# Memory attention: the sample's pair scores in the other PSUM pool, the prompt's last turn ahead of the value products, the convolution's small loads behind the output projection's weights

## The chip, the cores and the metric

The kernel runs on one core of a Trainium2 chip. The metric is the device time of one execution in microseconds (us); of several runs the median is taken. Engines are named as the profile names them: PE (TensorE matmul), PEld (its weight loads), DVE (VectorE), ACT (ScalarE), POOL (GpSimd) and SP (SyncE, which here issues nearly all DMAs).

## What is computed

One layer of a hybrid decoder, for a prompt group (512 rows) and a sample group (8 sequences of 4 rows) with the same weights: a mixer (mLSTM and differential attention), cross-attention into 256 memory tokens, and a convolutional FFN. The change lies in the cross-attention and at its seam to the FFN. Cut to what matters there:

```
def mem_attend(h, mk, mv, w_mq, w_mo):            # 4 heads x 256
    q = (h @ w_mq).reshape(B, T, MEM_HEADS, MEM_HEAD_DIM)
    s = jnp.einsum('bqhd,bkhd->bhqk', q, mk) * (MEM_HEAD_DIM ** -0.5)
    p = jax.nn.softmax(s, axis=-1)
    o = jnp.einsum('bhqk,bkhd->bqhd', p, mv).reshape(B, T, D_MODEL)
    return o @ w_mo

def conv_ffn(h, conv_buf, w_up, w_dw, b_dw, w_down):
    u = h @ w_up
    ext = jnp.concatenate([conv_buf, u], axis=1)
    c = b_dw
    for j in range(CONV_W):                       # 3 taps
        c = c + ext[:, j:j + T] * w_dw[j]
    a, g = c[..., :D_FF], c[..., D_FF:]
    return (jax.nn.silu(g) * a) @ w_down
```

The prompt's keys and values are computed from its memory; the sample's eight sequences each read their own keys and values (`cache_mem_k`, `cache_mem_v`, 1 MB each per sequence).

## The kernel before, in words

All products are float32: each weight tile of 512 KB is loaded into a staging tile (`wst`), ACT casts its high part (L146) and DVE subtracts to get the low part (L147); the pair is a `wslot`, of which there are four. A prompt product is three matmuls: high by high (L411), high by low (L412), low by high (L413).

PSUM has eight banks in two pools: `psm`, five banks, for tiles made by `mmp()`, and `psa`, three banks, for tiles made by `at()`. A tile takes a bank when one is free, and its first writer waits for the last reader of the tile that had the bank.

The memory attention has two strands that are woven together on PE:

- The prompt, one generator `prompt` with steps over eight items (4 heads x 2 row halves). Step t runs `ch_out(t-3)` (the product with the values, tile `cpo`, then the split into the projection's operand `oT`, for every second item 12 matmuls), `ch_turn(t-2)` (four transposes, tile `cpt`, then the splits `pT`), and `ch_soft(t)` (scores, tile `sca`, then DVE's maximum `cnm`, ACT's exponential `cp`, DVE's scaling of `cp`).
- The sample: `mk_scores` for pairs of sequences (tile `ssc`, one per sequence, L1527, copied by ACT to `sc`, L1530), `mk_sum` and `mem_softmax` (tiles `pS`, `spc`, `spt`; the weights end in `caz`), and `mv_out`, the products with the sample's values (tile `pso`, L1593) in the order `VORD`: sequences 2, 1, 0, then 7, 6, 5, 4, 3. The values of sequences 0 to 2 lie in the six staging tiles that weights use, those of 3 to 6 in the four buffers that `wslot` uses, those of 7 elsewhere.

After that come the first half of the projection by `w_mo` (tile `mm`), the transposes `ost` of the sample's result, and the transposes `cvp` (L1688, L1692) of the convolution's taps and states, which 24 small DMAs (L1674 to L1676) have brought into the tile `cr`. `xb` are five loads of the residual rows (L1144).

The order on each engine is set when the program is built: a scheduler takes the instructions by priority (mostly the order in which the code issues them), with two overrides, `tc.high_priority()` and `tc.issue_after(ins)`, which puts a block's instructions behind `ins` on its engine. Each engine, and the DMA queue of SP, then runs its list in that order. SP's DMAs use eight semaphores in turn, so that each waits for the landing of the one eight before it. `W` plans the weight slots; `W.pump()` issues what the slots allow, here four tiles of `w_mo`.

Of the kernel before, what the change touches and what calls it, by code (L numbers as in the profile page):

```python
# [15 lines left out]
P = 128  # L16
# [61 lines left out]
def kernel(ctx: ExitStack, tc: tile.TileContext, I, O):  # L78
# [9 lines left out]
    KSTEPS, VLOADS, NMID, VSTEPS = (3, 7, 11, 15), (13, 15), 3, (0, 1, 3, 5, 6, 7)  # L88
# [25 lines left out]
    def at(name="at"):  # L114
        return psa.tile([P, 512], F32, name=name, tag="at")

    def mmp(name="mm"):
        return psm.tile([P, 512], F32, name=name, tag="mm")
# [8 lines left out]
    def v2(t, b):  # L127
        return t.rearrange("p (a b) -> p a b", b=b)
# [10 lines left out]
    dma = nc.sync.dma_start  # L139
# [4 lines left out]
    def split(hi, lo, src, eng=None):  # L144

        nc.scalar.copy(out=hi, in_=src)  # L146
        (eng or nc.vector).tensor_tensor(out=lo, in0=src, in1=f32(hi), op=SUB)  # L147

    def rows(b):
        return (b * P, P) if b < 4 else (SEQ, NS)  # L150
# [56 lines left out]
    W = Weights(NSLOT)  # L207

    def stage():
        return stg.tile([P, 1024], F32, name="wst", tag="st")  # L210

    def slot_tile():
        return wp.tile([P, 2, 1024], F32R, name="wslot", tag="W")
# [11 lines left out]
    def slotA(w, k0, n0, nrow=256, share=False):  # L225
        def emit():
            st, s = v2(stage(), 512), slot_tile()
            sv = s.rearrange("p l (k n) -> p l k n", k=2)
            r0 = k0 * P
            if nrow == 256:  # L230
                dma(out=st, in_=w[r0:r0 + 256, n0:n0 + 512].rearrange("(k p) n -> p k n", p=P))
                split_w(sv, st, share)
            else:
                dma(out=st[:, 0, :], in_=w[r0:r0 + P, n0:n0 + 512])
                for p0 in (0, 64):
                    dma(out=st[p0:p0 + 64, 1, :], in_=w[r0 + P:r0 + P + 64, n0:n0 + 512])
                split(sv[:, 0], sv[:, 1], st)
            return sv, st
        W.add(emit)
# [113 lines left out]
    class Fill:  # L353
# [8 lines left out]
        def run(self, amount=1e9):  # L362
            while amount > 0 and self.q:
                try:
                    amount -= next(self.q[0])
                except StopIteration:
                    self.q.pop(0)
# [303 lines left out]
    for c0, c1 in HALF:  # L671
        n = c1 - c0
        ps = mmp()
# [51 lines left out]
    ps = at("gtp")  # L725
# [3 lines left out]
    ps = at("gtp")  # L729
# [193 lines left out]
    ps = at("npt")  # L923
# [37 lines left out]
    ps = at("nT0")  # L961
# [34 lines left out]
    ps = at("nTt")  # L996
# [122 lines left out]
    def proj_add(xt, gname, src, gname2, dst, order=None, scale=None):  # L1119

        g = gbc(gname)
        y0, s0, xb, pend, ready, target, late = {}, {}, {}, [], [], [], []

        def ssq(b, y, nm):
            n = rows(b)[1]
            ss = sm.tile([P, 1], F32, name=nm, tag=nm, bufs=6)
            j = Z("sqj")
            ACT(out=j[:n], in_=y, func=AF.Square, scale=DM ** -0.5, accum_out=ss[:n])
            return ss[:n]

        def ev0(b, ps):
            n = rows(b)[1]
            z = y0[b] = T2([P, 512], "y0")[:n]
            if b == 4:
                sample_sum(ps, z)
                ps = z
            s0[b] = ssq(b, ps, "ssy0")
            VTT(out=z, in0=ps, in1=g[:n, :512], op=MUL)

        def before(b):  # L1140
            for c in [4, 0, 1, 2, 3] if scale else [b]:
                if c not in xb:
                    xb[c] = N("xb")[:rows(c)[1]]
                    dma(out=xb[c], in_=src(c))  # L1144

        def ev1(b, ps):
            c0, n = rows(b)
            z = T2([P, 512], "y1")[:n]
            if b == 4:
                sample_sum(ps, z)  # L1150
                ps = z
            ss = ssq(b, ps, "ssy1")
            VTT(out=z, in0=ps, in1=g[:n, 512:], op=MUL)
            STT(out=ss, in0=s0[b], scalar=EPS, in1=ss, op0=ADD, op1=ADD)
            rs = rstd(ss, n, 1, None)
            late.append((b, z, rs))
            if not scale:
                add(*late.pop(0))

        def add(b, z, rs):  # L1160
            c0, n = rows(b)
            x = xb[b]
            for i, z in enumerate((y0[b], z)):
                c = slice(512 * i, 512 * i + 512)
                STT(out=x[:, c], in0=z, scalar=rs, in1=x[:, c], op0=MUL, op1=ADD)  # L1165
            dma(out=dst[c0:c0 + n, :], in_=x)
            ready.append((x, n, c0))
            while len(ready) > LR:
                rows_of(*ready.pop(0))

        def rows_of(x, n, c0):
            if scale is None:
                pend.append((norm_rows(x, n, ACTROWS), n, gname2, target[0], c0, POOLQ))
                return
            pend.append((x, n, gname2, target[0], c0, POOLQ))
            rs = sm.tile([P, 1], F32, name="rsd", tag="rsd", bufs=5)
            VCP(out=rs[:n], in_=rstd(sumsq(x, n, Z("sqx").bitcast(BF16)[:n]), n, 1, DM))
            scale[1].append((rs[:n], c0, n))

        def mid():  # L1180
            if len(pend) > (0 if scale else LP):
                norm_turn(*pend.pop(0))
            if late:

                with tc.issue_after(scaled[0].ins) if late[0][0] == 2 else nullcontext():
                    add(*late.pop(0))

        def second(xt2):
            target.append(xt2)
            run(gemmA(xt, 8, [4, 0, 1, 2, 3], ev1, block_major=True, before=before, mid=mid, midk=1 if scale else MIDK))  # L1190
            while late:
                add(*late.pop(0))
            while ready:
                rows_of(*ready.pop(0))
            while len(pend) > 2:
                norm_turn(*pend.pop(0))
            return pend
        return gemmA(xt, 8, order or allb, ev0, block_major=order is not None, halves=True), second
# [10 lines left out]
    for b in range(4):  # L1209
        c = slice(b * P, b * P + P)  # L1210
# [86 lines left out]
    prompt = pipe(4 * H, da_soft, lambda i: None, da_turn, da_av, da_end)  # L1297
# [59 lines left out]
    ps = at("dat")  # L1357
# [32 lines left out]
    for q in range(2):  # L1390
        st = v2(stage(), 256)
        dma(out=st, in_=mk_d[:, 4 * q:4 * q + 4])
        split(mkT[0][:, 4 * q:4 * q + 4], mkT[1][:, 4 * q:4 * q + 4], st)
    for c in range(2):
        st = stage()
# [113 lines left out]
    def mk_scores(bs):  # L1509

        t = None
        ps = {b: mmp("ssc")[:, :256] for b in bs}
        for e in range(2):
            if e and bs[0] == 0:
                next(prompt)
                t = scored[0].ins
            for b in bs:
                o = ps[b][:, e * P:e * P + P].rearrange("p (h c t) -> p h c t", h=2, c=2)
                for c in range(2) if b < 3 else (None,):
                    for j in range(8):  # L1520
                        g = NS * (j % 4)
                        if c is None:
                            w, k = o[g:g + NS], view(kst[b][0], 512 * e + NS * j, [(256, 2), (DM, 2), (1, NS)])
                        else:
                            w, k = o[g:g + NS, :, c], view(kst[b][c], 512 * e + NS * j, [(256, 2), (1, NS)])
                        with burst(t):
                            t = mm(w, lhsT=qx[e][j // 4][:, j % 4, b].rearrange("p e g t -> p (e g t)"), rhs=k,  # L1527
                                   start=(j < 4), stop=(j >= 4)).ins
        for b in bs:
            nc.scalar.copy(out=sc[:, b], in_=ps[b])  # L1530
        return t
# [80 lines left out]
    prompt = steps()  # L1612
# [30 lines left out]
    mk_sum(t)  # L1643
    with tc.high_priority():
        mem_softmax()
    for _ in range(NMID):
        next(prompt, None)
    pso = mmp("pso")[:, :256]
    for n0 in (0, 512):
# [1 line left out]
    W.nslots = NSLOT  # L1651
    mv_out(VORD[:6])
    W.pump()
    next(prompt, None)
    next(prompt, None)
    mv_out(VORD[6:])
    run(prompt)
    oS = Z("oS")[:, :256]
    nc.scalar.copy(out=oS, in_=pso)
    ps = at("ost")  # L1660
    for e in range(2):
        tr(ps[:, e * P:(e + 1) * P], oS[:, e * P:(e + 1) * P], ident)
    ps = ps[:, :256].rearrange("p (e h n) -> p h e n", e=2, n=NS)
# [8 lines left out]
    def conv_in(t, p0, o, c0, n):  # L1672

        dma(out=t[p0:p0 + 16, o:o + n], in_=conv0[:, c0:c0 + n])  # L1674
        dma(out=t[p0 + 16:p0 + 19, o:o + n], in_=I["w_dw"][0][:, c0:c0 + n])
        dma(out=t[p0 + 19:p0 + 20, o:o + n], in_=I["b_dw"][:, c0:c0 + n])  # L1676


    cr = N("cr")
    for g in range(6):  # L1680
        conv_in(cr, 20 * g, 0, 896 * g + (64 if g > 2 else 0), 896)
    conv_in(cr, 0, 896, 2688, 64)
    conv_in(cr, 0, 960, 5440, 64)
    for t0 in (0, 4):
        ps = at("cvp")
        nt = min(4, 7 - t0)
# [4 lines left out]
    ps = at("cvp")  # L1691
# [33 lines left out]
    def spread(i):  # L1725
# [9 lines left out]
        if i == 0:  # L1735
# [3 lines left out]
                            scale=(rsb, rss))  # L1739
# [109 lines left out]
    for gi, js in enumerate(groups):  # L1849
# [49 lines left out]
        if not last:  # L1899
            behind = []  # L1900
            for n0 in (0, 512):
# [3 lines left out]
                ps = [mmp() for _ in range(4)]  # L1905
# [11 lines left out]
            ps = {n0: at("sdn") for n0 in (0, 512)}  # L1917
# [141 lines left out]
```

## Time and profile before

| what | value |
|---|---|
| median of 3 runs | 939.27 us (938.86 to 941.57) |
| the profiled execution | 938.97 us |
| its span, first to last instruction | 937.2 us |
| PE busy | 914.7 us (98% of the span) |
| mean granted TensorE clock | 0.994 |
| HBM traffic | 138 GB/s over the span |

A profile is one execution. A row of the timeline gives the start, the busy time, the engine, the line and the operands; in brackets stands the idle time of the engine before it and what ended that. `x12` means twelve instructions merged into one row; a float32 matmul that isn't split by the kernel has two records. On SP a row is the time of issuing, not of the transfer. In a table of stretches the columns are the stretch, its length, the busy time with the number of instructions, the granted clock, the share of busy DMA engines and GB/s.

### The profile page before, as it was taken

The page shows a single profiled execution, that of the slowest core. Times are in us where ns is not written, and L with a number is a line of the kernel's source. Part 1 is how long each engine was busy: PE and PEld are TensorE (multiplying, and loading weights), DVE is VectorE, ACT ScalarE, POOL GpSimd, SP SyncE. Part 2 cuts the span into 40 slices and gives each one's busy share as a digit, 9 for nine tenths or more (in the row PEclk, how much of TensorE's full clock was granted, in tenths as well). Part 3 has the DMA queues.
Part 4 walks back from the last instruction along what each step waited for, and adds up shares of the span by engine and source line. Part 5 has one row for each costly group of instructions (what it writes and reads, how often), then busy time and mean ns, then how long its engine had stood idle before and what let it go on. Part 6 is the DMA issues. An engine that isn't in the chain of part 4 may idle for free. (4 is left out here: it accounts for less than half of the span.)

```text
span 937.2 us, 17472 instructions
## 1 busy us (share of the span) xinstructions
PE 914.7 (98%) x6780; PEld 798.0 (85%) x6780; DVE 607.5 (65%) x1128; ACT 377.7 (40%) x728; POOL 223.4 (24%) x475
## 2 busy tenths in 40 slices
PE   8999999999999999999999999999999999999995
PEld 5899787879866778998767899889988998999974
DVE  5845144565887438687545778637747785776767
ACT  5745233344586447724434533332212222222232
POOL 6611000024442116581000553001100110110114
PEclk9999999999999999999999999999999999999998
DMA  8950023335780439956766632062054304412023
GB/s 282 320 182 5 1 90 138 91 105 159 246 294 7 137 117 299 321 189 232 283 231 166 202 116 69 26 180 69 22 140 133 89 10 116 133 49 90 24 94 118
DMA packets 120834, 130.59 MB, mean 139 GB/s; under 512 B 8599, under 2 KB 86264, under 8 KB 120752
## 3 DMA queue, kind: packets, MB, share of 16 engines
q1 hardware_dynamic: 114568, 125.96, 42.5%
q10 hardware_dynamic: 6184, 3.53, 1.2%
q8 instruction: 53, 0.87, 0.4%
q14 instruction: 29, 0.24, 0.1%
HBM read 112.54 MB, written 16.93 MB: 138 GB/s over the span
## 5 line engine op out<-in xcount | busy, mean ns | idle before, releaser
L146 ACT CAST wslot<-wst 128x1024 fp32r<-128x1024 f32 x125 | 130.7, 1049 | 265.5 <-issue 72.6
L485 PE MATMUL mm<-fT,wslot 128*128 128x256 f32 x1872 | 235.9, 288 | 0.0
L485 PEld LDWEIGHTS mm<-fT,wslot 128*128 128x128 f32 x1872 | 234.4, 188 | 1.8 <-issue 0.8
L147 DVE TENSOR_TENSOR wslot<-wst,wslot 128x1024 fp32r<-128x1024 f32 x125 | 154.5, 1239 | 85.4 <-ACT wslot L146 84.8
L1865 PE MATMUL mm<-wslot,act 128*128 128x512 f32 (+1 forms) x180 | 69.3, 387 | 0.0
L1868 PE MATMUL mm<-wslot,act 128*128 128x512 f32 (+1 forms) x172 | 67.1, 391 | 0.0
L1869 PE MATMUL mm<-wslot,act 128*128 128x512 f32 (+1 forms) x172 | 66.8, 392 | 0.0
L1767 POOL COPY cvo<-u 128x2 f32<-128x2 f32 x43 | 10.4, 242 | 217.1 <-DVE u L1765 217.1
L411 PE MATMUL mm<-wslot,hT 128*128 128x512 f32 x128 | 51.3, 402 | 0.0
L413 PE MATMUL mm<-wslot,hT 128*128 128x512 f32 x128 | 51.0, 399 | 0.0
L485 PE MATMUL mm<-hT,wslot 128*128 128x256 f32 (+1 forms) x384 | 50.9, 289 | 0.0
L412 PE MATMUL mm<-wslot,hT 128*128 128x512 f32 x128 | 50.8, 397 | 0.0
L1762 DVE TENSOR_TENSOR u<-mm,rsb 128x256 f32<-128x256 f32 x43 | 18.1, 423 | 48.8 <-PE mm L485 48.7
L485 PEld LDWEIGHTS mm<-hT,wslot 128*128 128x128 f32 x384 | 49.2, 188 | 0.5 <-issue 0.2
L1865 PEld LDWEIGHTS mm<-wslot,act 128*128 128x128 f32 x180 | 34.3, 191 | 8.0 <-issue 0.8
L1869 PEld LDWEIGHTS mm<-wslot,act 128*128 128x128 f32 x172 | 32.3, 188 | 6.9 <-issue 0.4
L1868 PEld LDWEIGHTS mm<-wslot,act 128*128 128x128 f32 x172 | 32.3, 188 | 6.9
L1779 ACT ACTIVATE c<-c 128x560 f32<-128x560 f32 x21 | 14.1, 672 | 56.8 <-DVE c L1773 56.7
L1773 DVE SCALAR_TENSOR_TENSOR c<-u,cvT,c 128x560 f32<-128x560 f32 x43 | 34.3, 798 | 0.9
L1772 DVE SCALAR_TENSOR_TENSOR c<-u,cvT,c 128x560 f32<-128x560 f32 x43 | 34.1, 793 | 0.2
L1880 DVE TENSOR_TENSOR yp<-mm,yp 128x512 f32<-128x512 f32 (+1 forms) x41 | 27.1, 673 | 4.8 <-PE mm L1869 4.6
L413 PEld LDWEIGHTS mm<-wslot,hT 128*128 128x128 f32 x128 | 24.1, 188 | 5.0
(497 smaller groups left out, 1859.1 us busy)
## 6 DMA issues: line engine op xcount, KB each, us to landing
wst<-in_w_up_dram SPq DMA_DIRECT2D x42, 512.0 KB
wst<-in_w_in_dram SPq DMA_DIRECT2D x28, 512.0 KB
wst<-in_w_down_dram SPq DMA_DIRECT2D x20, 512.0 KB
kvt<-in_cache_mem_k_dram SPq DMA_DIRECT2D x10, 512.0 KB
kvt<-in_cache_mem_v_dram SPq DMA_DIRECT2D x10, 512.0 KB
wst<-in_w_mk_dram SPq DMA_DIRECT2D x8, 512.0 KB
xb<-in_x_prompt_dram SPq DMA_DIRECT2D x8, 512.0 KB
wst<-in_cache_dk_dram SPq DMA_DIRECT2D x16, 256.0 KB
```

The source lines that it names most:

```text
L146: nc.scalar.copy(out=hi, in_=src)
L147: (eng or nc.vector).tensor_tensor(out=lo, in0=src, in1=f32(hi), op=SUB)
L411: mm(ps[b], lhsT=xt.hi(k, c0, c0 + n), rhs=s[:, 0, kk, :], start=(k == 0), stop=False)
L412: mm(ps[b], lhsT=xt.hi(k, c0, c0 + n), rhs=s[:, 1, kk, :], start=False, stop=False)
L413: return mm(ps[b], lhsT=xt.lo(k, c0, c0 + n), rhs=s[:, 0, kk, :], start=False, stop=(k == nk - 1))
L485: mm(ps[i], lhsT=s[:, l, k, :], rhs=x(k, c0, c1), start=(k == 0 and j == 0), stop=(k == 7 and j == 2))
L1772: STT(out=c, in0=u[:, 1:EXT - 1], scalar=w[1], in1=c, op0=MUL, op1=ADD)
L1773: STT(out=c, in0=u[:, 0:EXT - 2], scalar=w[0], in1=c, op0=MUL, op1=ADD)
L1865: mm(ps, lhsT=t[:, 0, c0:c0 + P], rhs=s[:, 0, i % 2, cs], start=st, stop=False)
L1868: mm(ps, lhsT=t[:, 0, c0:c0 + P], rhs=s[:, 1, i % 2, cs], start=False, stop=False)
L1869: return mm(ps, lhsT=t[:, 1, c0:c0 + P], rhs=s[:, 0, i % 2, cs], start=False, stop=en)
L1880: VTT(out=y, in0=ps, in1=y, op=ADD)
```

## The change

It has three parts. First, `mk_scores` takes its two tiles `ssc` from `at()` (three banks) and no longer from `mmp()` (five). Second, the steps of the prompt that are left after the softmax are issued earlier: four of them, not three, ahead of the first value products, and all the rest ahead of the second group of value products. Third, the small loads of the convolution and the five loads `xb` are put behind the last of the `w_mo` loads that `W.pump()` has issued, by `tc.issue_after`; for this the load is kept in `W.last`.

```
             if nrow == 256:
-                dma(out=st, in_=w[r0:r0 + 256, ...])
+                W.last = dma(out=st, in_=w[r0:r0 + 256, ...])
...
                 if c not in xb:
                     xb[c] = N("xb")[:rows(c)[1]]
-                    dma(out=xb[c], in_=src(c))
+                    with tc.issue_after(loads) if scale else nullcontext():
+                        dma(out=xb[c], in_=src(c))
...
     def mk_scores(bs):
-        ps = {b: mmp("ssc")[:, :256] for b in bs}
+        ps = {b: at("ssc")[:, :256] for b in bs}
...
-    for _ in range(NMID):
+    for _ in range(NMID + 1):
         next(prompt, None)
     pso = mmp("pso")[:, :256]
...
     mv_out(VORD[:6])
     W.pump()
-    next(prompt, None)
-    next(prompt, None)
+    loads = W.last.ins
+    run(prompt)
     mv_out(VORD[6:])
-    run(prompt)
...
     cr = N("cr")
-    for g in range(6):
-        conv_in(cr, 20 * g, 0, 896 * g + (64 if g > 2 else 0), 896)
-    conv_in(cr, 0, 896, 2688, 64)
-    conv_in(cr, 0, 960, 5440, 64)
+    with tc.issue_after(loads):
+        for g in range(6):
+            conv_in(cr, 20 * g, 0, 896 * g + (64 if g > 2 else 0), 896)
+        conv_in(cr, 0, 896, 2688, 64)
+        conv_in(cr, 0, 960, 5440, 64)
```

Lines after L1143 have numbers that are higher by one in the changed kernel (L1660 to L1676 have the same ones; L1688 becomes L1689).

The first place is PE in the scores of the first pair: sequence 1 (`ssc_5162`), then a turn (`cpt`) and the scores of the next prompt item (`sca`). In brackets stand the engines that a row waits for. Before:

```order
L1527 MATMUL ssc_5162<-wst_4797,qx_4474 32x2x32 [waits DVE_49]
L1527 MATMUL ssc_5162<-wst_4797,qx_4474 32x2x32 x3
L1527 MATMUL ssc_5162<-wst_4797,qx_4475 32x2x32 x4
L1527 MATMUL ssc_5162<-wst_4798,qx_4474 32x2x32 x4
L1527 MATMUL ssc_5162<-wst_4798,qx_4475 32x2x32 x4
L1473 MATMUL cpt_5195<-cpk_87,cp_5068 128x128 [waits DVE_49]
L1473 MATMUL cpt_5195<-cpk_87,cp_5068 128x128 x3
L1454 MATMUL sca_5204<-mkT_4453,qh_4486 128x256 [waits DVE_49,Activation_49]
```

The same rows now:

```order
L1528 MATMUL ssc_5162<-wst_4797,qx_4474 32x2x32 x4
L1528 MATMUL ssc_5162<-wst_4797,qx_4475 32x2x32 x4
L1528 MATMUL ssc_5162<-wst_4798,qx_4474 32x2x32 x4
L1528 MATMUL ssc_5162<-wst_4798,qx_4475 32x2x32 x4
L1474 MATMUL cpt_5195<-cpk_87,cp_5068 128x128 [waits DVE_49,Activation_49]
L1474 MATMUL cpt_5195<-cpk_87,cp_5068 128x128 [waits DVE_49]
L1474 MATMUL cpt_5195<-cpk_87,cp_5068 128x128 x2
L1455 MATMUL sca_5204<-mkT_4453,qh_4486 128x256 [waits DVE_49]
```

The order is the same; the wait of `ssc_5162` for DVE and that of `sca_5204` for ACT are gone, and the turn now waits for its own operand `cp` of DVE and for ACT's last reading of its bank.

The second place is PE from the sample's weights (`spt`) to the first products of the output projection (`mm`). Before:

```order
L1573 MATMUL spt<-cpk,spc 32x32 x32
L1593 MATMUL pso<-wst,caz 32x256 x24
L1473 MATMUL cpt<-cpk,cp 128x128 x4
L1593 MATMUL pso<-kvt,caz 32x256 x40
L1485 MATMUL cpo<-pT,mvN 128x512 x12
L411 MATMUL mm<-wslot,oT_5340 128x512 x2
```

Now:

```order
L1574 MATMUL spt<-cpk,spc 32x32 x32
L1474 MATMUL cpt<-cpk,cp 128x128 x4
L1594 MATMUL pso<-wst,caz 32x256 x24
L1486 MATMUL cpo<-pT,mvN 128x512 x12
L1594 MATMUL pso<-kvt,caz 32x256 x40
L411 MATMUL mm<-wslot,oT_5340 128x512 x4
```

The last turn stands ahead of the first value products, the last prompt products ahead of the second ones, and the projection follows the second value products directly.

The third place is the DMA queue of SP behind the sample's values (`kvt`). Before, its end is:

```order
L1674 DMA cr<-in_state_conv_dram 16x64
L1675 DMA cr<-in_w_dw_dram 3x64
L1676 DMA cr<-in_b_dw_dram 1x64
L1144 DMA xb<-x_d_2551 32x1024
L1144 DMA xb<-x_d_2551 128x1024
L231 DMA wst<-in_w_mo_dram 128x2x512 x6
L1144 DMA xb<-x_d_2551 128x1024 x3
L231 DMA wst<-in_w_mo_dram 128x2x512 x2
```

Now it begins with:

```order
L1584 DMA kvt<-in_cache_mem_v_dram 128x1024 x10
L231 DMA wst<-in_w_mo_dram 128x2x512 x4
L1674 DMA cr<-in_state_conv_dram 16x896
L1675 DMA cr<-in_w_dw_dram 3x896
L1676 DMA cr<-in_b_dw_dram 1x896
```

All 24 small loads and two of the `xb` loads stood ahead of the first `w_mo` load; now four `w_mo` loads stand ahead of them, and after the 24 small loads come two more of `w_mo`, the five `xb` and the last two of `w_mo`. On PE the first `cvp` transposes now stand behind 26 matmuls of the projection, where there were 13.

More of the change, by code (lines that the diff above doesn't have):

```diff
@@ L230, in emit @@
             if nrow == 256:
-                dma(out=st, in_=w[r0:r0 + 256, n0:n0 + 512].rearrange("(k p) n -> p k n", p=P))
+                W.last = dma(out=st, in_=w[r0:r0 + 256, n0:n0 + 512].rearrange("(k p) n -> p k n", p=P))
                 split_w(sv, st, share)
```

## The prediction

> **What bounds the kernel now.** I read the page's summary first, then PE's waits by stretch, then the granted clock and the timeline around the change.
>
> ```profile
> span 937.2 us, 17472 instructions
> ...
> PE 914.7 (98%) x6780; PEld 798.0 (85%) x6780; DVE 607.5 (65%) x1128; ACT 377.7 (40%) x728; POOL 223.4 (24%) x475
> ```
>
> PE is the bound, so only PE's idle time and slow time are to be had. Its waits from 425 to 500 us, the whole neighbourhood of the change, are these; the last row is all that it waits from 498 us to the end:
>
> ```profile
> PE mm L411 <- ACT wslot L146: 1.4, 1, 1.4
> PE sca L1454 <- ACT cp L1461: 1.1, 1, 1.1
> PE pso L1593 <- ACT caz L1576: 0.6, 1, 0.6
> PE ssc L1527 <- DVE ql L1438: 0.6, 1, 0.6
> PE mm L412 <- DVE wslot L147: 0.5, 1, 0.5
> ...
> PE mm L472 <- ACT fT L146: 0.3, 1, 0.3
> ```
>
> So 4.2 us are idle here, and what PE gains here arrives at the end nearly whole: later stages wait for PE, not PE for them. The stretches add a second loss, the clock:
>
> ```profile
> 432.00:436.00 4.00, 2.31 (x72) 1.00 0.63 247
> ...
> 474.96:478.24 3.28, 1.38 (x5) 1.00 1.03 385
> 478.24:481.65 3.41, 3.41 (x10) 0.50 1.05 402
> ```
>
> After a stretch in which PE was busy for 1.38 of 3.28 us, the clock is 0.50 for 3.41 us. The timeline of PE shows where:
>
> ```profile
> 462.75 0.76 PE L1573 MATMUL spt<-cpk,spc 128*32 128x32 f32 x64
> 464.14 2.80 PE L1593 MATMUL pso<-wst,caz 128*32 128x256 f32 x48 [0.62 <-ACT caz L1576]
> 466.87 0.66 PE L1473 MATMUL cpt<-cpk,cp 128*128 128x128 f32 x4
> 467.45 4.52 PE L1593 MATMUL pso<-kvt,caz 128*32 128x256 f32 x80
> 471.91 3.05 PE L1485 MATMUL cpo<-pT,mvN 128*128 128x512 f32 x12
> 476.33 0.73 PE L411 MATMUL mm<-wslot,oT 128*128 128x512 f32 x2 [1.38 <-ACT wslot L146]
> 477.59 0.50 PE L412 MATMUL mm<-wslot,oT 128*128 128x512 f32 x1 [0.53 <-DVE wslot L147]
> ...
> 481.80 0.38 PE L1662 MATMUL ost<-cpk,oS 128*128 128x128 f32 x2
> ...
> 483.21 0.40 PE L413 MATMUL mm<-wslot,oT 128*128 128x512 f32 x1
> 483.44 0.40 PE L411 MATMUL mm<-wslot,oT 128*128 128x512 f32 x1
> ```
>
> PE stands still at the projection's first product, because its first weight comes late. ACT's casts and SP's queue show why:
>
> ```profile
> 475.24 1.04 ACT L146 CAST wslot<-wst 128x1024 fp32r<-128x1024 f32 x1 [6.44 <-DMA wst<-in_w_mo_dram]
> 476.51 1.05 ACT L146 CAST wslot<-wst 128x1024 fp32r<-128x1024 f32 x1 [0.23 <-DMA wst<-in_w_mo_dram]
> ...
> 479.26 1.04 ACT L146 CAST wslot<-wst 128x1024 fp32r<-128x1024 f32 x1 [0.33 <-DMA wst<-in_w_mo_dram]
> ...
> 464.12 0.32 SPq L1674 DMA_DIRECT2D cr<-in_state_conv_dram  x1
> ...
> 467.78 0.25 SPq L1676 DMA_DIRECT2D cr<-in_b_dw_dram  x1
> 468.13 0.78 SPq L1144 DMA_DIRECT2D xb<-x_d  x2
> 469.00 4.96 SPq L231 DMA_DIRECT2D wst<-in_w_mo_dram  x6
> ```
>
> SP issues the first weight at 469.00, after the small loads and two `xb`; it lands at about 475.24, and the following ones every 1.3 us (475.24 to 479.26 in three steps).
>
> **The weights ahead of the small loads.** The first weight now waits for its staging tile alone, which the first of six groups of value products frees: 464.14 + 2.80/6 = 464.6. Its time from issue to landing lies between 6.24 us (469.00 to 475.24, behind other traffic) and the nearest row of a load on a quiet queue, near the end of the kernel:
>
> ```profile
> 899.91 0.90 SPq L231 DMA_DIRECT2D wst<-in_w_down_dram  x2
> ...
> 903.67 1.04 ACT L146 CAST wslot<-wst 128x1024 fp32r<-128x1024 f32 x1 [9.31 <-DMA wst<-in_w_down_dram]
> ```
>
> That is 3.76 us, which I take, because here too the queue has drained by then (SP issues its last small load without a wait). The first weight lands at 468.4, the fourth at 472.4.
>
> **The products in another order.** The turn (0.58 us of PE from 466.87 to 467.45) goes into the gap of 0.62 us before 464.14. Its operand is ready:
>
> ```profile
> 461.67 0.61 DVE L1464 TENSOR_SCALAR cp<-cp,csu 128x256 f32<-128x256 f32 x2
> ```
>
> It ends at 462.28, the gap starts at 463.5. Gain between 0 and 0.6; I take 0.55. Then the values' first group ends at 466.87 as before, the 12 prompt products (about 2.9) end at 469.8, and the second group (4.46) runs from 469.8 to 474.2, where the projection follows. Now `cpo` no longer covers the casts, so their cover has to be named: the slots are buffers of the values 6, 5, 4, 3, and that group reads 7 first and 6 next. The first slot is free after 16 of 40 products, at 471.6; ACT's cast (1.05) ends at 472.6, DVE's subtraction (about 1.24, by the page's groups) at 473.9, and the next casts follow by 1.05 each; ACT's and DVE's splits of `cpo` are done by 471.2. All of this is before 474.2, hidden under the second value group.
>
> ```profile
> L146 ACT CAST wslot<-wst 128x1024 fp32r<-128x1024 f32 x125 | 130.7, 1049 | 265.5 <-issue 72.6
> ...
> L147 DVE TENSOR_TENSOR wslot<-wst,wslot 128x1024 fp32r<-128x1024 f32 x125 | 154.5, 1239 | 85.4 <-ACT wslot L146 84.8
> ```
>
> So the wait of 1.38 goes whole. From 476.33 to 481.80 PE did 13 products in 5.47 us; at 0.23 each (483.21 to 483.44) they take 3.0, so 2.47 more go: 0.53 of the second wait, 1.7 of the half clock (3.41 x 0.5), and 0.24 of refilling. Together 3.85; I take 3.8. The bounds are 0.5 and 3.85, the lower one from the rivals.
>
> The clock is where a rule speaks against this. The Trainium skill ("TensorE: Matmul & The Clock Gate", "Why this matters for your kernels") says that the clock falls after idle gaps of more than about 3 us. The two gaps here are 1.38 and 0.53 us, so by that rule they wouldn't be the cause, the half clock would stay, and the term would be 2.1. The trace doesn't agree as far as it goes: the slow stretch begins right behind the only 3.3 us in which PE was idle for more than half.
>
> **The small loads behind the weights.** This is the cost. With eight in flight, four small loads go out at once, the next four wait for one weight each, so that sixteen are left when the fourth weight lands at 472.4. From 464.12 to 467.78 SP issued eleven in 3.66 us without a wait, 0.33 each: the last goes out at 472.4 + 5.3 = 477.7. No row gives a small load's landing; since with eight in flight none waited, it is under 8 x 0.33 = 2.6, so all are in by 478 to 480.3. PE comes to `cvp` after 26 products and `ost`, 474.2 + 6.0 + 0.4 = 480.6. With the weight's landing at its other end (6.24), the small loads are in at 482.8 and PE waits 2.2. Cost 0 to 2.2; I take 0.1, by the quiet-queue row. Queued behind them on SP are the fifth and sixth weight and the five `xb`; the second half of the projection needs those only after 96 products (22 us), and the last `xb` waited for the last `cvp` before too. The last two weights wait for the sample's products as before.
>
> **The scores.** Both waits were for banks of the five-bank pool:
>
> ```profile
> 433.47 0.65 PE L1527 MATMUL ssc<-wst,qx 128*32 128x64 f32 x32 [0.62 <-DVE ql L1438]
> 434.05 0.66 PE L1473 MATMUL cpt<-cpk,cp 128*128 128x128 f32 x4
> 435.78 0.50 PE L1454 MATMUL sca<-mkT,qh 128*128 128x256 f32 x2 [1.07 <-ACT cp L1461]
> ...
> 440.19 3.06 PE L1485 MATMUL cpo<-pT,mvN 128*128 128x512 f32 x12
> ...
> 432.50 0.57 DVE L1464 TENSOR_SCALAR cp<-cp,csu 128x256 f32<-128x256 f32 x2
> 432.99 0.75 DVE L1438 SCALAR_TENSOR_TENSOR ql<-mm,qh 128x256 fp32r<-128x256 f32 x2
> ...
> 438.95 0.42 DVE L147 TENSOR_TENSOR pT<-cpt,pT 128x256 fp32r<-128x256 f32 x1
> ```
>
> With `ssc` in the other pool, sequence 1 follows without the 0.62; the turn then starts at 433.4 with its `cp` ready at 433.07, and `sca` takes a bank that the first of the two subtractions at 432.99 frees by 433.4, so the 1.07 goes too. What is late next is DVE's split at 438.95, done at 439.37, which the fifth `cpo` product needs: 1.69 earlier it would start at 438.50 + 1.0 = 439.5, just behind it. So the gain is capped near 1.7. Below stands a loss: three banks for the pairs tie each second pair to ACT's copies of the first, and the nearest row of such a wait is 1.07. Bounds -1.1 and 1.7; I take 1.6, since each operand named has its row.
>
> **The sum.** 1.6 + 0.55 + 3.8 - 0.1 = 5.85 us, so the profiled execution goes from 938.97 to 933.1 (span 931.35); the median of the runs stands 0.3 above it, which gives 933.4.
>
> **Rivals.**
> 1. The scores gain nothing, because the waits come back at the turn or at ACT's copies: 933.4 + 1.6 = 935.0. For it speaks that the turn now waits for DVE and ACT; against it that both rows end 0.3 us earlier.
> 2. The half clock has another cause and stays: 935.1. The skill's rule above gives this time; for it speaks that 432 to 436 us, with 1.69 us idle in 4.0, kept the full clock; against it that those gaps were spread wider and PE was still busy for more than half.
> 3. `cvp` waits for the small loads: up to 2.2, 935.6, if weights land as slowly as before.
> 4. The slots come free in the wrong order, so that the first cast starts at 474.2: PE then waits about 1.35 (cast and the low part) and keeps 0.5 of the 1.9, with or without the clock: 935.1 to 936.8, say 936. Against it: the first cast's buffer is named above.
> 5. The other side: the small loads become the bound. They end 7.9 us (5.3 + 2.6) after the fourth weight. If that lands no earlier than before (479.26), they are in at 487.2, PE waits 6.6 at `cvp`, the clock halves again (1.7), and 5.85 gained becomes 2.4 lost: 941.7. It takes a landing after about 477 to decide, against 472.4 worked out.
>
> **Chances.** The forecast 0.57; rivals 1 to 4: 0.12, 0.08, 0.10, 0.06; rival 5: 0.04; nothing moves: 0.03. A measurement can tell about 0.3%, 2.8 us, so faster is below 936.4: 0.57 + 0.12 + 0.08 + 0.10 and half of rival 4, 0.89 with rounding; within 0.3% 0.07, slower 0.04. The range reaches from 931.9 (the scores' and the clock's terms somewhat larger, and the spread of the runs) to 936.0, the end of rival 3 and the middle of 4.
>
> **What would show it.** In the changed kernel's profile: no wait of `ssc` for `ql` nor of `sca` for `cp` near 433 us; the first `w_mo` load issued right after the first value products and landed before the second group; no wait at the first `mm` product; a granted clock of 1.00 from there on; `cvp` with no wait for `cr`. I am wrong if PE waits at `cvp`, if a stretch at 0.50 remains, or if the casts still end after the second value group.

## The result, and the profile after

The changed kernel takes 934.20 us (median of 5 runs, 933.29 to 935.08) against 940.53 for the kernel before beside it: a ratio of 0.9933, 95% interval 0.9919 to 0.9947, so 0.67% faster, 5.0 to 7.6 us. The forecast was 933.4, with a range of 931.9 to 936.0. The profiled execution of the changed kernel took 934.94 us, longer than three of the other four; its span is 4.0 us shorter than that of the execution profiled before, and where the other two microseconds are is part of what follows.

The summary of the page, the waits of PE from 425 to 500 us, and the granted clock in three stretches of 3.41 us at the projection (columns: stretch, length, PE busy and its instructions, granted clock, DMA share, GB/s):

```profile
span 933.2 us, 17471 instructions
...
PE 912.8 (98%) x6780; PEld 797.2 (85%) x6780; DVE 607.1 (65%) x1128; ACT 377.9 (40%) x728; POOL 224.6 (24%) x475
```
```profile
PE ssc L1528 <- issue: 0.7, 1, 0.7
PE sca L1455 <- issue: 0.2, 1, 0.2
```
```profile
471.46:474.87 3.41, 3.41 (x61) 1.00 0.56 188
474.87:478.29 3.42, 3.42 (x16) 1.00 0.25 66
478.29:481.70 3.41, 3.41 (x22) 1.00 0.22 64
```

The five waits of before, 4.2 us, are gone, with two small new ones of 0.65 and 0.16 us for which the profile names no releaser. PE is busy without a break through the projection's start, at the full clock. Its timeline, with one row of ACT, shows the new order:

```profile
436.51 1.31 PE L1528 MATMUL ssc<-wst,qx 128*32 128x64 f32 x77
437.29 0.76 ACT L1531 COPY sc<-ssc 128x256 f32<-128x256 f32 x2
438.47 0.47 PE L1528 MATMUL ssc<-wst,qx 128*32 128x64 f32 x18 [0.65 <-issue]
...
463.04 0.76 PE L1574 MATMUL spt<-cpk,spc 128*32 128x32 f32 x64
463.73 0.66 PE L1474 MATMUL cpt<-cpk,cp 128*128 128x128 f32 x4
464.43 2.80 PE L1594 MATMUL pso<-wst,caz 128*32 128x256 f32 x48
467.16 3.06 PE L1486 MATMUL cpo<-pT,mvN 128*128 128x512 f32 x12
470.15 4.52 PE L1594 MATMUL pso<-kvt,caz 128*32 128x256 f32 x80
474.60 1.21 PE L411 MATMUL mm<-wslot,oT 128*128 128x512 f32 x4
...
480.53 0.38 PE L1662 MATMUL ost<-cpk,oS 128*128 128x128 f32 x2
...
480.99 0.88 PE L1689 MATMUL cvp<-cpk,cr 120*128 120x120 f32 x7
```

The queue of SP and ACT's casts show what stands behind it:

```profile
465.13 1.92 SPq L231 DMA_DIRECT2D wst<-in_w_mo_dram  x4
467.14 0.71 SPq L1674 DMA_DIRECT2D cr<-in_state_conv_dram  x1
...
474.14 0.24 SPq L1675 DMA_DIRECT2D cr<-in_w_dw_dram  x1
...
479.35 0.25 SPq L1676 DMA_DIRECT2D cr<-in_b_dw_dram  x1
479.70 0.90 SPq L231 DMA_DIRECT2D wst<-in_w_mo_dram  x2
...
472.15 3.90 ACT L146 CAST wslot<-wst 128x1024 fp32r<-128x1024 f32 x4 [1.31 <-PE pso L1594]
```

The first weight is issued at 465.13, where it was 469.00. The cast at 472.15 no longer waits for a DMA but for PE's value products, which free its slot: the weights are early. SP's own waits date the landings: four of the small loads wait for one weight each and are issued at 469.20, 470.49, 472.12 and 474.14, so the first weight was in 3 us ahead of its cast, and the fourth about 0.9 us ahead of the last of the four casts. The small loads go out until 479.6, and `cvp` at 480.99 does not wait for them.

And one loss ahead of the change, on PE and DVE:

```profile
416.68 3.14 PE L485 MATMUL mm<-hqT,wslot 128*128 128x288 f32 x23 [1.21 <-DVE ql L1439]
```
```profile
412.22 1.25 DVE L1508 STREAM_TRANSPOSE wst<-wst 128x1024 f32<-128x1024 f32 x1 [0.67 <-DMA wst<-in_cache_mem_k_dram]
415.07 1.25 DVE L1508 STREAM_TRANSPOSE wst<-wst 128x1024 f32<-128x1024 f32 x1 [1.60 <-DMA wst<-in_cache_mem_k_dram]
416.24 0.71 DVE L1439 SCALAR_TENSOR_TENSOR ql<-mm,qh 128x256 fp32r<-128x256 f32 x2
```

PE waited 1.21 us for DVE, which stood at a transpose whose keys landed late. The order of the instructions on PE, DVE, POOL and SP is the same in both kernels up to there, and the kernel before had no such wait in its profile; the experiments show whose it is.

### The profile page after: what moved, and what is told of

Read it like the earlier page. It is cut to its first block, busy times and chain, and to the rows that moved or that the text cites. A ratio compares the mean times of both kernels' runs of the same rounds, so it can differ in the third digit from the quotient of the medians.

```text
span 933.2 us, 17471 instructions
## 1 busy us (share of the span) xinstructions
PE 912.8 (98%) x6780; PEld 797.2 (85%) x6780; DVE 607.1 (65%) x1128; ACT 377.9 (40%) x728; POOL 224.6 (24%) x475
## 5 line engine op out<-in xcount | busy, mean ns | idle before, releaser
L411 PE MATMUL mm<-wslot,hT 128*128 128x512 f32 x128 | 51.3, 402 | 0.0
L412 PE MATMUL mm<-wslot,hT 128*128 128x512 f32 x128 | 50.9, 397 | 0.0
```

The costliest lines, as they stand in the source:

```text
L411: mm(ps[b], lhsT=xt.hi(k, c0, c0 + n), rhs=s[:, 0, kk, :], start=(k == 0), stop=False)
L412: mm(ps[b], lhsT=xt.hi(k, c0, c0 + n), rhs=s[:, 1, kk, :], start=False, stop=False)
```

## The experiments

To compare profiles that start unequally, the table gives the length of five stretches of each profiled execution, worked out from the starts of rows in PE's timeline: from the first pair's scores (`ssc`) to the first `cpo`; to the first value products (`pso`); to the projection's first product (`mm`); to the first `rsb` (a tile with the row factors of the FFN's normalisation) behind the projection; to the end of the span. "Start" is the time of the first `ssc`. "Half" tells whether a half clock stands at the projection.

| kernel | start | ssc to cpo | cpo to pso | pso to mm | mm to rsb | rsb to end | half |
|---|---|---|---|---|---|---|---|
| before | 432.19 | 8.00 | 23.95 | 12.19 | 55.02 | 405.84 | yes |
| before, 2nd profile | 432.49 | 7.98 | 23.91 | 12.05 | 55.00 | 406.86 | yes |
| before, 3rd profile | 434.80 | 7.93 | 23.95 | 12.37 | 54.03 | 406.31 | no |
| scores only | 433.67 | 6.57 | 23.93 | 12.61 | 55.00 | 406.38 | yes |
| order only | 433.06 | 7.97 | 23.95 | 11.32 | 53.01 | 406.12 | no |
| loads only | 432.01 | 7.96 | 23.95 | 10.65 | 52.61 | 406.30 | no |
| without scores | 434.19 | 7.98 | 23.91 | 10.16 | 52.51 | 406.03 | no |
| without order | 432.91 | 6.72 | 23.95 | 10.64 | 52.60 | 406.01 | no |
| after | 433.48 | 6.77 | 24.18 | 10.17 | 52.53 | 406.03 | no |
| after, again | 432.90 | 6.73 | 23.93 | 10.15 | 52.51 | 406.02 | no |

The stretches from `ssc` to `rsb` repeat within some 0.3 us wherever the same part of the change is in and the clock is the same. The start, up to which all these programs are the same, scatters over 2.8 us, and the end of the kernel before over 1.0, so the times of single executions can't be compared more closely than that.

**Scores only.** The pool of `ssc` alone:

```diff
-        ps = {b: mmp("ssc")[:, :256] for b in bs}
+        ps = {b: at("ssc")[:, :256] for b in bs}
```

> Only the pool of the pair scores is changed. Theory A (the gain is carried on): the transfers of the sample's values start when the scores free their buffers (SP issued the first at 437.88 us before, 437.00 after) and run back to back from there, so w_mo lands earlier by as much as the scores end earlier; gain 0.9 to 1.6 us, and the wait of the projection's first product stays near 1.4. Theory B (the weight sets the pace): w_mo lands at 475.2 us whatever the scores do, the 1.6 gained early is waited out at the projection (1.38 grows to about 3), gain 0. Theory C (the scores gain nothing at all): ssc and sca lose their waits but wait elsewhere before 445 us; gain 0, with cpo starting at about 440.2 us as before.

Measured: 938.15 against 939.75 us, ratio 0.9983 (0.9968 to 0.9998). The stretch from `ssc` to `cpo` shortens by 1.43 us, and the wait at the projection grows:

```profile
PE mm L411 <- ACT wslot L146: 1.8, 1, 1.8
```

So 0.42 of the 1.43 is waited out, and 1.0 is left against the profiled execution of before. That is nearer theory A than B, though the wait grew to 1.81 where A had it stay near 1.4. Theory C falls.

**Order only.** The last turn and `cpo` ahead, the loads where they were:

```diff
-    for _ in range(NMID):
+    for _ in range(NMID + 1):
...
     W.pump()
-    next(prompt, None)
-    next(prompt, None)
-    mv_out(VORD[6:])
     run(prompt)
+    mv_out(VORD[6:])
```

> Only the prompt's last turn and last products are moved ahead. Theory A (the parts hang together): the first w_mo load still stands behind the small loads on SP and lands at about 475.2 us, so the 0.55 to 0.64 us that the turn saves is waited out at the projection's first product (1.38 becomes about 2.0), the clock is halved there as before, and the time moves by 0 to 0.4 us. Theory B (each part gains its own term): 0.55 us faster. Theory C: without the prompt's products as cover the casts come late, 1 us slower or more.

Measured: 938.11 against 939.75, ratio 0.9980 (0.9966 to 0.9993), 1.6 us by medians and 1.9 by the ratio: more than any of the three said. The first product still waits for the weight, yet the clock stays whole (same columns as above, the stretch with the wait and the next):

```profile
469.69 3.24 SPq L231 DMA_DIRECT2D wst<-in_w_mo_dram  x6
475.21 1.04 ACT L146 CAST wslot<-wst 128x1024 fp32r<-128x1024 f32 x1 [3.81 <-DMA wst<-in_w_mo_dram]
476.30 1.20 PE L411 MATMUL mm<-wslot,oT 128*128 128x512 f32 x4 [1.08 <-ACT wslot L146]
```
```profile
474.10:477.52 3.42, 2.32 (x28) 1.00 1.02 371
477.52:480.93 3.41, 3.37 (x15) 1.00 1.05 390
```

In the stretch from `mm` to `rsb` it is 1.0 us shorter than the third profile of before (below), whose clock was whole too. The order also changes how the scheduler lays out the projection: four L411 products stand ahead of the first L412, so that its 0.53 us wait for DVE is covered, and `ost` and `cvp` stand behind 25 products and no longer 13. The expectation had left out both. Nor did the wait grow to 2.0, as theory A had it: the first weight was cast 5.52 us after its issue, where it was 6.24 before. One profile doesn't show whether that is the order's doing or chance.

**Loads only.** The small loads and `xb` behind the fourth weight (the `issue_after(loads)` blocks of the change, the rest as before):

> Only the small convolution loads and the xb loads are put behind the fourth w_mo load. Theory A: this part alone brings the 3.8 us of the projection (1.38 and 0.53 of waits, 1.7 of half clock, 0.24 of refilling), clock 1.00 throughout until the end of the kernel, no wait at cvp. Theory B (the half clock has another cause than PE's idle time): a stretch of about 3.4 us at 0.50 remains and the gain is 2.1. Theory C (the small loads become late): cvp waits up to 2.2 us and the gain is 1.6 to 3.

Measured: 936.50 against 939.75, ratio 0.9964 (0.9947 to 0.9982). 1.54 us go from `pso` to `mm`, 2.41 from `mm` to `rsb`, 3.95 together where 3.8 was expected, against the profiled execution of before with its half clock; against the third profile, without one, it is 3.14, and by the medians 3.25. There is no wait at the projection or at `cvp` and no half clock there: theory A, with a gain that depends on what it is compared with.

**Without the scores; without the order; the changed kernel again.** Each with one part of the change undone:

> The changed kernel with the pair scores back in the five-bank pool. Theory A (the scores' term is about 1.2 to 1.4, as the stretch from the first pair's scores to cpo shortened from 8.00 to 6.77 and 6.57 us in two kernels): 1.0 to 1.4 us slower than the changed kernel, so 4.3 to 4.9 faster than before, with the 0.6 and 1.07 waits back. Theory B (the scores' gain was given back at once, by the new waits of 0.65 and 0.16 us): as fast as the changed kernel within 0.3 us.

> The changed kernel with the prompt's last turn and products back behind the value products. Theory A (the order and the loads overlap: either alone kept the clock, and with the loads early the weights are there without it): only the turn's 0.6 us is lost, so 5.0 to 5.3 us faster than before. Theory B (the order's 1.9 us adds to the others): 1.9 us slower than the changed kernel, 4.0 faster than before.

> The changed kernel itself, beside the others on one chip. Theory A (the sum of the forecast, with 1.2 in place of 1.6 for the scores): 5.4 us faster than before. Theory B (the profiled execution, 4.0 faster, is the usual one, and the wait of 1.21 us at 416.7 us belongs to the change): 4.0 faster, and the profile shows that wait again at more than 1 us.

Measured on one chip against 939.83 us: without the scores 935.69, ratio 0.9959 (0.9946 to 0.9972); without the order 935.86, ratio 0.9962 (0.9946 to 0.9978); the changed kernel 934.17, ratio 0.9936 (0.9921 to 0.9951). Undoing the scores costs 1.5 us by medians and 1.25 in the stretches (7.98 against 6.73), with its waits back:

```profile
PE sca L1454 <- ACT cp L1461: 1.1, 1, 1.1
PE ssc L1527 <- DVE ql L1438: 0.6, 1, 0.6
```

For the scores that is theory A. Undoing the order costs 1.7 by medians, but in the stretches only 0.49 (10.64 against 10.15) and 0.09 behind it; the start accounts for nothing (432.91 and 432.90), and the profiled executions differ by 0.60 (934.61 and 934.01). The medians alone are nearer B (4.0 faster than before), but each is uncertain by over 1 us and they don't settle it; the stretches, of one execution each, speak for A. For the changed kernel, the sum from `ssc` to `rsb` is 93.32 us where before's was 99.16: 5.84 less.

**The subtractions ahead of the transposes.** The changed kernel, with the last two transposes of the staged keys behind two `ql` on DVE:

```diff
-            mk_turn(i // 4)
+            with tc.issue_after(qls[9].ins) if i == 9 else nullcontext(): mk_turn(i // 4)
```

> The changed kernel, with the last two transposes of the staged keys put behind two ql subtractions on DVE that were ready long before (PE waited 1.21 us at 416.7 us for them in the changed kernel's profile, 0.2 to 0.5 in others, none in the kernel before). Theory A (that wait comes with keys that land late, on some executions): no wait of mm for ql there, the fastest executions unchanged, the median 0.2 to 0.6 us faster than the changed kernel. Theory B (the subtractions wait for something else): the wait stays and the time is the same.

Measured: 933.78 against 939.83 us, ratio 0.9931 (0.9916 to 0.9947), 0.4 below the changed kernel and within its interval. In its profile the keys came late again, and PE did not wait:

```profile
412.50 1.07 DVE L1439 SCALAR_TENSOR_TENSOR ql<-mm,qh 128x256 fp32r<-128x256 f32 x3
413.74 1.25 DVE L1508 STREAM_TRANSPOSE wst<-wst 128x1024 f32<-128x1024 f32 x1 [0.16 <-DMA wst<-in_cache_mem_k_dram]
416.32 1.25 DVE L1508 STREAM_TRANSPOSE wst<-wst 128x1024 f32<-128x1024 f32 x1 [1.34 <-DMA wst<-in_cache_mem_k_dram]
```
```profile
413.81 6.39 PE L485 MATMUL mm<-hqT,wslot 128*128 128x288 f32 x50
```

So the wait of 1.21 us comes from keys that land late in some executions and from DVE's order, not from the change: it stands with 0.97 us without the scores, 0.69 without the order, 0.69 in the changed kernel's second profile, 0.46 with the order alone, and 1.2 in the third profile of before, where nothing was changed. Whether the cure moves the median is not shown.

**The filled gap.** Does PE's idle time halve the clock? The kernel before, with five products of `cpo`'s kind in the gap ahead of the projection:

```diff
     run(prompt)
+    fp = at("fill")
+    for _ in range(5):
+        mm(fp, lhsT=mvN[0][:, 1, 7 * P:8 * P], rhs=pTs[3][1][0], start=True, stop=True)
```

> The kernel before, with five extra prompt products (128x512, 0.23 us each, their result is never read) on PE between the last cpo product and the projection's first product, in the 1.38 us in which PE waits for the first weight. The wait for the weight itself is not touched. Theory A (the idle time halves the clock): PE is busy for over 60% of that stretch, the clock stays 1.00 and the kernel is faster by about 1.7 us (1.2 to 2.0) although it does more work. Theory B (the half clock comes from something else): the 3.4 us at 0.50 remain and the time is the same or up to 0.3 us slower.

Measured: 940.34 (median of 11; a twelfth execution took 1006.27) against 939.75, ratio 1.0007 (0.9994 to 1.0021). The clock stayed at 1.00, and no time was gained: a result that neither theory had. The scheduler had moved `ost` from behind 13 products to behind 8, and there PE waited:

```profile
480.61 0.44 PE L1662 MATMUL ost<-cpk,oS 128*128 128x128 f32 x2 [1.13 <-ACT oS L1659]
```

ACT copies `oS` (at 480.19) behind its casts of the late weights (the fourth at 479.23). Two things had changed at once, so the fill was tried again in a place where the order of everything else stays as it was: between the sample's weights and the first value products, with 14 and with 8 products of 128x256.

```diff
+    for _ in range(14): mm(fp[:, :256], lhsT=mvN[0][:, 1, 7 * P:8 * P], rhs=pTs[3][1][0][:, :256], start=True, stop=True)
```

> The kernel before, with 14 extra products of 128x256 (0.13 us each, 1.83 in all; their result is never read) on PE between the sample's weights and the first value products; no other instruction changes its place. They fill the 0.62 us gap there and push all that follows by 1.2 us, so that the wait of 1.38 at the projection's first product shrinks to about 0.2, while the weight lands when it did. Theory A (the idle time halves the clock, and the half clock costs time by itself): clock 1.00 there, ost at 480.2 to 480.6 in place of 481.80, 1.2 to 1.6 us faster with 14 products more. Theory B (the late weights and ACT's copies hold PE there whatever its clock is): clock 1.00 too, but a wait of more than 1 us before ost, and the time within 0.3 us of before.

> The same with 8 extra products (1.05 us): the wait at the projection's first product shrinks to about 0.95, beside 0.53 behind it. Theory A (the clock of one stretch of 3.41 us is set by PE's busy share in the stretch before it, with the step at about a half: 0.44 and 0.33 were followed by 0.50, 0.53 and 0.68 by 1.00): the share is about 0.57, the clock stays 1.00, and the gain is that of 14 products, 1.2 to 1.6 us. Theory B (any gap of about 1 us or more at that place halves it): 0.50 for 3.41 us, no gain.

With 14, measured: 940.27 against 939.58, ratio 1.0009 (0.9997 to 1.0020). Its profile does what theory A said, with no wait at the first product, a short one at `ost`, and the clock at 1.00:

```profile
465.57 1.93 PE L1657 MATMUL fill<-pT,mvN 128*128 128x256 f32 x14 [0.28 <-ACT pT L146]
467.43 2.80 PE L1593 MATMUL pso<-wst,caz 128*32 128x256 f32 x48
...
478.08 0.62 PE L411 MATMUL mm<-wslot,oT 128*128 128x512 f32 x2
...
482.19 0.44 PE L1662 MATMUL ost<-cpk,oS 128*128 128x128 f32 x2 [0.20 <-ACT oS L1659]
```

From `ssc` to `rsb` it is 97.85 us, 1.3 less than the profiled execution of before (99.16) although PE does 1.93 more of work. But the medians show none of the gain that theory A had: they are 0.7 us slower (the interval reaches from 0.3 faster to 1.9 slower), and theory B had the same time within 0.3. With 8 (939.57 against 939.58, ratio 0.9996, 0.9983 to 1.0009) the clock stays whole at the projection, and is halved in another place, at the scores, whose waits are those of before:

```profile
433.22:436.63 3.41, 1.61 (x61) 1.00 0.63 250
436.63:440.05 3.42, 3.42 (x36) 0.50 0.00 0
```

Here `ssc` to `cpo` takes 9.60 us where it takes 8.0 at the full clock. With waits of the same size the order-only profile kept it, its stretch being busy for 1.81 us:

```profile
433.14:436.55 3.41, 1.81 (x68) 1.00 0.66 264
436.55:439.96 3.41, 3.35 (x124) 1.00 0.23 19
```

Both fills left a question: if a filled gap saves 1.3 us against the profile of before, why not in the medians? One answer would be that the profiled execution, with its half clock, is not the usual one: over the 72 executions of the kernel before that ran beside these kernels, 22 had a mean clock of 0.994 or less, like the profiled one, and 50 had 0.995 or more. So the kernel before was profiled twice more.

> The kernel before, unchanged, profiled once more. Theory A (the half clock at the projection belongs to some executions: of 72 executions of this kernel 22 had a mean clock of 0.994 or less, as the profiled one, and 50 had 0.995 or more; one stretch of 3.41 us at 0.50 takes 0.002 off the mean): the waits of 1.38 and 0.53 stand there again, and whether the clock halves goes by how the two lie in the stretches of 3.41 us; most likely 1.00, with about 54.0 us from the projection's first product to its last in place of 55.1. Theory B (it always halves there): 0.50 for 3.41 us and 55.1 us again.

> The same kernel, a second look. Theory A: as in the first look, with whole or half clock by the busy share of the stretch (under about a half is followed by 0.50), here or at the scores' two waits near 433 us; the sum of all else is the same within 0.5 us apart from what lies ahead of the scores. Theory B: half clock at the projection in both looks.

The second profile (940.07 us): the stretch with the two waits and the next, then the first of the waits:

```profile
474.27:477.68 3.41, 1.65 (x7) 1.00 1.02 386
477.68:481.10 3.42, 3.42 (x8) 0.50 1.06 389
```
```profile
476.43 0.72 PE L411 MATMUL mm<-wslot,oT 128*128 128x512 f32 x2 [1.23 <-ACT wslot L146]
```

The third (941.16 us):

```profile
475.80:479.21 3.41, 1.86 (x9) 1.00 0.98 344
479.21:482.63 3.42, 2.89 (x12) 1.00 1.04 388
```
```profile
479.05 0.73 PE L411 MATMUL mm<-wslot,oT 128*128 128x512 f32 x2 [1.55 <-ACT wslot L146]
480.31 0.50 PE L412 MATMUL mm<-wslot,oT 128*128 128x512 f32 x1 [0.53 <-DVE wslot L147]
483.30 0.44 PE L1662 MATMUL ost<-cpk,oS 128*128 128x128 f32 x2 [0.17 <-ACT oS L1659]
```

The longer wait (1.55) left the clock whole and the shorter (1.23) halved it: what differs is how the waits lie in the stretches of 3.41 us. Theory A holds, one execution each way, though the whole clock that it called most likely came in one look of two, and the stretch behind the projection differs by 1.0 us between the three profiles where 0.5 was expected. The half clock is worth 1.0 us at the projection (55.00 against 54.03). How many executions have it there is not shown: two of the three profiled ones do, and the second of them has a mean clock of 0.995, so the count by mean clocks doesn't tell. Nor is the question of the fills settled. Against the third profile the 14 products save 0.4 us and not 1.3 (97.85 against 98.28), but the medians don't show that either.

## Why the prediction was right

**The total.** 933.4 was forecast and 934.20 measured. The stretches bear the sum out: 5.84 us less from `ssc` to `rsb` in the changed kernel's second profile, 5.51 in its first, 5.85 forecast. Against the third profile of before, with its clock whole, they give 5.0 (98.28 - 93.32) and 4.6. So the gain is 4.6 to 5.8, mostly by whether the execution of before had the half clock. All of that lies in the interval of the second measurement (5.7, from 4.6 to 7.4), and what is above 5.0 in that of the first (6.3). The first two profiles differ by 4.0 in their spans and not by 5.5, because `ssc` starts 1.29 later in the changed kernel's, with the wait of 1.21 for `ql` in it, and the end is 0.2 longer; the one execution ran 1.6 below the median of 940.53, the other 0.7 above its own. That the time itself came out is in part luck. It was counted from one execution that had the half clock but an early start, and from 939.27, the lowest of that kernel's medians (939.58 to 940.53 in the others).

**The scores, 1.6.** Measured 1.27 and 1.23 in the two profiles of the changed kernel, 1.43 alone. The step that was too large is the claim that no wait follows: at 438.47 PE stood still for 0.65 us (0.41 to 0.65 in every profile with this part), which no row of before had shown and for which the profile names no releaser. The forecast's lower bound had named ACT's copies `sc`, which free the banks of the pair; but PE went on 0.18 to 0.42 us after the end of the second copy, not at a fixed time behind it, so the cause stays open. In the first profile, and in that with the subtractions ahead, a second such wait of 0.16 to 0.17 near 451.5 went with 0.2 to 0.3 us more from `cpo` to `pso`. Rival 1 (nothing gained) falls.

**The turn into the gap, 0.55.** 0.49, from 10.64 to 10.15 between `pso` and `mm`. The turn is at 463.73 and `pso` follows it without a wait.

**The weights, 3.8.** 3.95 with the loads alone, 4.55 with the order too, less 0.49 for the turn: 4.06, against the profiled execution of before; with the loads alone against the third profile, 3.14. The links stand, each a little late: the first weight issued at 465.13 (464.6 forecast) and in by 469.20 (468.4), 4.07 us later, near the 3.76 of the quiet queue; the first cast at 472.15 (471.6) and released by `pso`; the first product at 474.60 (474.2). PE was 0.29 us late already at `spt`. Only the pace of the weights was misjudged: the next three came 1.29, 1.63 and 2.02 us apart, where 1.3 was taken, and the cover of the second value products was long enough for that. Rival 4, slots freed in the wrong order, falls.

**The clock, 1.7 of that.** This term was mis-sized in two ways that the total hides. It was 1.0 in the one pair of profiles that shows it. Part of the difference is a wait that the slow products had covered (`ost` for ACT, 0.17 to 0.20); the rest is not worked out. And it is a matter of some executions: the profiled one of before had it, and also had an early start (432.19; the others run to 434.80), which made up for it. Rival 2, another cause, falls: the clock was whole at the projection in every kernel in which early weights or a fill took the gap away, and in the order-only kernel with a gap of 1.08. The Trainium skill's rule that stood for that rival ("TensorE: Matmul & The Clock Gate", "Why this matters for your kernels", gaps of more than about 3 us) is not what the traces show: half clocks followed stretches whose longest gap was 1.07, 1.23, 1.38 and 1.81 us.

**The small loads, 0.1 of cost.** Nothing: no profile with this part shows a wait of `cvp`. The last of them is issued at 479.35, where 477.7 was forecast, since the fourth weight was in at 474.14 and not at 472.4; the sixteen loads behind it took 5.2 us (5.3 forecast). `cvp` comes at 480.99 (480.6) and finds them landed. Rivals 3 and 5 fall.

## What to carry to other kernels

When a transfer that opens a stage stands behind many small ones on its queue, move the small ones, and name the work that will cover them: alone that brought 3.25 of the 5.66 us here (medians). Read a gain from stretches between the same two rows of several profiles; single executions of the kernel before differed by 2.6 us ahead of the place of the change. A half clock in one profile is a property of that execution until other profiles show it again, and a mean clock doesn't tell where it fell: remove the gap for its own sake, and don't count the half clock as a cost of every execution.

## What the runs showed of the hardware that was not expected

The granted clock is decided in stretches of 3.41 us: each half clock inside the kernel lasted 3.41 us and began at a whole number of such stretches from the clock's first record. In the middle of the kernel, PE's busy time in one stretch told the clock of the next, with the step at about a half: 1.14 of 3.42 us (scores only, whose rows follow), 1.50 (before, 474.81 to 478.22), 1.61 and 1.65 were followed by 0.50; 1.81, 1.86 and 2.32 by 1.00. From 40 to 900 us no stretch in any of the profiles goes against this. No single gap decided it. It held less well at the ends: a share of 0.60 at 9.5 us was followed by 0.50 in the kernel without the scores and by 1.00 in the third profile of before, at 8.2 us; and 1.64 of 3.41 us at 924.8 us was followed by 1.00 in the second profile of before.

```profile
475.02:478.44 3.42, 1.14 (x4) 1.00 0.99 353
478.44:481.85 3.41, 3.41 (x10) 0.50 1.05 382
```

The Trainium skill ("TensorE: Matmul & The Clock Gate", "Part 1: The HAM clock gate (the "warmup" mystery)") states a free-running window of 3413 ns; the trace agrees with its length, 3.41 us, and with a phase that differs from one execution to the next. That a stretch idle for half is enough is what the runs here add.
